# An encoder block on one core: merged moving operands in the block products, a last stage by token tile, and another order of the first loads

## The chip, the core and the metric

The kernel runs on one core of one Trainium2 chip. The metric is the device time of one execution in microseconds (us); the time given is the median of several runs. A profile is one execution, recorded instruction by instruction. Engines: PE is TensorE (matmuls) and PEld its weight loads, DVE is VectorE, ACT is ScalarE, POOL is GpSimd, SP is SyncE, which issues most DMAs.

## The reference, cut to what matters

```python
def reference(x, norm_mix, w_in, ..., norm_ffn, w_gate, w_up, w_down, norm_final):
    h = rmsnorm(x, norm_mix)                 # x: 512 tokens x 2048
    z = h @ w_in                             # Fourier part a, gMLP parts u and v
    ...
    x = x + concatenate([y_f, y_g]) @ w_out
    h2 = rmsnorm(x, norm_ffn)
    x = x + (silu(h2 @ w_gate) * (h2 @ w_up)) @ w_down    # d_ff = 5632
    return rmsnorm(x, norm_final)
```

Everything is float32. The weights `w_gate`, `w_up` (2048 x 5632) and `w_down` (5632 x 2048) carry most of the work.

## The kernel before

**Precision.** A float32 product is made of three matmuls in a reduced type (fp32r). Each operand is split into `hi` (a cast by ACT, L173) and `lo` (the rest, a subtraction by DVE, L174); then hi times hi, lo times hi and hi times lo are added up in one PSUM bank. So every weight tile of 128 x 1024 costs ACT one cast and DVE one subtraction, whatever is done with it.

**Stages, in order of time.** The input projections, the two mixers and the output projection (to about 560 us). Then the feed-forward part, an item list that `drive` (L925) walks: 16 plain gate and up units (`GateUp`); 16 pairs of **block products** (`Matrix`, `Block`: one gate matrix, one up matrix a pair, 32 of the 44 feature tiles); the rest of the gate and up units mixed with 140 `Product` items, the block products of the down projection, whose results POOL's DMA adds into DRAM (L818, `accum_op=ALU.add`); and at the end the down projection's last four feature tiles, done plainly (`Last` and the loop behind `drive`), with the final norm.

**A block product** works on a 2 x 2 cut of one matrix with seven products in place of eight (Strassen's scheme in Winograd's form). Sums of weight blocks are made by DVE in place (`sums`, L629), four a matrix, from four loaded blocks (L626). A product has 8 contraction tiles, and in each the three matmuls of `mm3b` (L700 to L702) with 256 moving columns, a token half: 24 matmuls. `out` (L661) takes the 256 columns of PSUM and combines them in the tiles `u`, `w` and `o`; at a pair's end `o` is scaled by the norm (L683, L685), passed through a silu and multiplied (L686), and stored by POOL's DMA (`keep`, L527).

**Order.** SP's, PE's, DVE's, ACT's and POOL's queues are written by hand in the feed-forward part: they hold the instructions in the order in which `drive` calls the items. At an item x, `drive` first makes the weight sums of the item three ahead (`sums`), then casts and splits the weights of the item two ahead (`prep`), issues loads further ahead (`load_ahead`), then calls `later` and `late` of the items before, then x's matmuls (`run`) and x's PSUM work (`out`). The `hi` and `lo` tiles have three buffers each, so a cast waits for PE to finish the item three earlier.

**The opening.** SP's queue holds the first half of the first activation tile, `g_mix`, then the first half of the first weights, and so on. ACT squares and casts in the order that a scheduler found.

**The end.** `Last(n)` multiplies one of the last two down units with all four token tiles and DVE adds the four results to x (L844). Then, token tile by token tile, the last unit is added (L970), squared with a row sum (L459), multiplied by the final gain (POOL, L973; the very last on DVE) and, when the row sums are there, by the inverse root (L112 to L118, L981, L983).

## Time and profile before

| | |
|---|---|
| median of 3 runs | 1850.15 us (1849.55 to 1850.80) |
| the profiled execution's own time | 1850.23 us |
| its span, first to last instruction | 1848.5 us |
| PE busy | 1820.0 us (98%), 10674 matmuls |
| DVE busy | 1407.4 us (76%) |
| ACT busy | 785.0 us (42%) |
| DMA, hardware queue | 209.83 MB, 33.7% of 16 engines |
| DMA, software (POOL) queue | 57.68 MB, 15.2% of 16 engines |

A matmul's duration in the trace is its way through the array; matmuls overlap, so what one costs is read from the distance of two starts. PEclk is the granted TensorE clock; 1.00 is the 2.4 GHz level. A row of a timeline gives start, duration, engine, line, operation and tiles, and in brackets the idle time of the engine before it with what ended it.

### The profile page before, as it was taken

The page shows a single profiled execution, that of the slowest core. Times are in us where ns is not written, and L with a number is a line of the kernel's source. Part 1 is how long each engine was busy: PE and PEld are TensorE (multiplying, and loading weights), DVE is VectorE, ACT ScalarE, POOL GpSimd, SP SyncE. Part 2 cuts the span into 40 slices and gives each one's busy share as a digit, 9 for nine tenths or more (in the row PEclk, how much of TensorE's full clock was granted, in tenths as well). Part 3 has the DMA queues.
Part 4 walks back from the last instruction along what each step waited for, and adds up shares of the span by engine and source line. Part 5 has one row for each costly group of instructions (what it writes and reads, how often), then busy time and mean ns, then how long its engine had stood idle before and what let it go on. Part 6 is the DMA issues. An engine that isn't in the chain of part 4 may idle for free.

```text
span 1848.5 us, 26416 instructions
## 1 busy us (share of the span) xinstructions
PE 1820.0 (98%) x10674; PEld 1614.0 (87%) x10674; DVE 1407.4 (76%) x1683; ACT 785.0 (42%) x1014; POOL 152.5 (8%) x160
## 2 busy tenths in 40 slices
PE   9999999999999999999999999999999999999996
PEld 7888888888888999999999999988888788788785
DVE  7554664333578888888888888889899898899957
ACT  6345533222333444443444444444445455444534
POOL 5001110000000000000000000001111111111104
PEclk9999999999999999999999999999999999999998
DMA  6322224442342343333334333338888878788672
GB/s 244 99 70 95 98 80 137 137 144 95 116 175 86 111 140 115 116 133 107 104 117 137 113 124 128 138 126 205 205 220 206 211 197 208 177 224 210 119 248 111
DMA packets 75577, 269.18 MB, mean 146 GB/s; under 512 B 8768, under 2 KB 8896, under 8 KB 75456
## 3 DMA queue, kind: packets, MB, share of 16 engines
q1 hardware_dynamic: 59616, 209.83, 33.7%
q0 software_dynamic: 15840, 57.68, 15.2%
q8 instruction: 83, 1.36, 0.3%
q14 instruction: 38, 0.31, 0.0%
HBM read 206.66 MB, written 60.82 MB: 145 GB/s over the span
## 4 chain that ended last, share of the span: by engine, by line
PE 89%; DVE 7%; issue 2%; ACT 1%; DMA 0%; POOL 0%; SPq 0%; ACTq 0%; DVEq 0%
PE upb L702 6%; PE upb L700 6%; PE upb L701 6%; PE gb L702 6%; PE gb L701 6%; PE gb L700 6%; PE d L790 5%; PE d L791 5%; PE d L789 5%; PE o L87 3%; PE o L85 3%; PE o L86 3%; PE g L87 2%; PE g L86 2%; PE g L85 2%; PE up L87 2%
## 5 line engine op out<-in xcount | busy, mean ns | idle before, releaser
L790 PE MATMUL d<-lo_d,X 128*128 128x512 f32 x560 | 219.4, 392 | 4.0 <-DVE lo_d L174 4.0
L789 PE MATMUL d<-hi_d,X 128*128 128x512 f32 x560 | 218.1, 389 | 2.4 <-DVE c L812 2.4
L791 PE MATMUL d<-hi_d,X 128*128 128x512 f32 x560 | 218.1, 389 | 0.0
L173 ACT CAST hi_d<-w 128x1024 fp32r<-128x1024 f32 x140 | 147.4, 1053 | 152.2 <-PE d L791 45.7
L174 DVE TENSOR_TENSOR lo_d<-w,hi_d 128x1024 fp32r<-128x1024 f32 x140 | 170.8, 1221 | 28.2 <-ACT hi_d L173 28.1
L173 ACT CAST hi_gb<-w_gb 128x1024 fp32r<-128x1024 f32 x112 | 117.5, 1049 | 150.0 <-PE upb L701 43.7
L173 ACT CAST hi_upb<-w_upb 128x1024 fp32r<-128x1024 f32 x112 | 117.5, 1050 | 135.4 <-PE gb L701 46.6
L174 DVE TENSOR_TENSOR lo_upb<-w_upb,hi_upb 128x1024 fp32r<-128x1024 f32 x112 | 136.8, 1221 | 37.3 <-ACT hi_upb L173 37.3
L174 DVE TENSOR_TENSOR lo_gb<-w_gb,hi_gb 128x1024 fp32r<-128x1024 f32 x112 | 136.7, 1221 | 34.4 <-ACT hi_gb L173 34.4
L702 PE MATMUL gb<-hf,lo_gb 128*128 128x256 f32 x512 | 145.0, 283 | 0.5 <-DVE lo_gb L174 0.5
L701 PE MATMUL gb<-hf,hi_gb 128*128 128x256 f32 x512 | 145.0, 283 | 0.4 <-DVE hf L174 0.4
L700 PE MATMUL gb<-hf,hi_gb 128*128 128x256 f32 x512 | 144.9, 283 | 0.0
L700 PE MATMUL upb<-hf,hi_upb 128*128 128x256 f32 x512 | 144.9, 283 | 0.0
L701 PE MATMUL upb<-hf,hi_upb 128*128 128x256 f32 x512 | 144.9, 283 | 0.0
L702 PE MATMUL upb<-hf,lo_upb 128*128 128x256 f32 x512 | 144.9, 283 | 0.0
L790 PEld LDWEIGHTS d<-lo_d,X 128*128 128x128 f32 x560 | 105.1, 188 | 30.8 <-DVE lo_d L174 9.3
L789 PEld LDWEIGHTS d<-hi_d,X 128*128 128x128 f32 x560 | 105.1, 188 | 25.1 <-ACT hi_up L173 2.0
L791 PEld LDWEIGHTS d<-hi_d,X 128*128 128x128 f32 x560 | 105.1, 188 | 21.3
L80 DVE TENSOR_TENSOR lo_o<-raw_o,hi_o 128x1024 fp32r<-128x1024 f32 x32 | 39.2, 1226 | 102.4 <-ACT hi_o L79 102.4
L700 PE MATMUL gb<-h2hi,hi_gb 128*128 128x256 f32 x384 | 108.8, 283 | 0.8 <-ACT t_gb L666 0.8
L702 PE MATMUL gb<-h2hi,lo_gb 128*128 128x256 f32 x384 | 108.8, 283 | 0.5 <-DVE lo_gb L174 0.5
L700 PE MATMUL upb<-h2hi,hi_upb 128*128 128x256 f32 x384 | 108.7, 283 | 0.0
(322 smaller groups left out, 4981.3 us busy)
## 6 DMA issues: line engine op xcount, KB each, us to landing
w<-in_w_down SPq DMA_DIRECT2D x80, 512.0 KB, 5.7
cd<-c POOLq DMA_DIRECT2D x80, 512.0 KB, 7.2
w_gb<-in_w_gate SPq DMA_DIRECT2D x64, 512.0 KB, 4.1
w_upb<-in_w_up SPq DMA_DIRECT2D x64, 512.0 KB, 4.4
raw_o<-in_w_out SPq DMA_DIRECT2D x32, 512.0 KB, 3.5
raw_g<-in_w_gate SPq DMA_DIRECT2D x24, 512.0 KB, 6.6
raw_up<-in_w_up SPq DMA_DIRECT2D x24, 512.0 KB, 6.8
ac<-ad SPq DMA_DIRECT2D x20, 512.0 KB, 3.6
```

The source lines that it names most:

```text
L80: nc.vector.tensor_sub(lo[:, c], raw[:, c], hi[:, c])
L85: mm(ps, lhs[0], rhs[0], start=first, stop=False)
L86: mm(ps, lhs[0], rhs[1], start=False, stop=False)
L87: mm(ps, lhs[1], rhs[0], start=False, stop=last)
L173: nc.scalar.copy(dst[0], src)
L174: nc.vector.tensor_sub(dst[1], src, dst[0])
L700: mm(ps, lhs[0], rhs[0], start=first, stop=False, skip_group_check=True)
L701: mm(ps, lhs[0], rhs[1], start=False, stop=False, skip_group_check=True)
L702: mm(ps, lhs[1], rhs[0], start=False, stop=last, skip_group_check=True)
L789: mm(p, X[:, 0, j, l], hi, start=j == 0 and not more, stop=False, skip_group_check=True)
L790: mm(p, X[:, 0, j, l], lo, start=False, stop=False, skip_group_check=True)
L791: mm(p, X[:, 1, j, l], hi, start=False, stop=j == 1, skip_group_check=True)
```

## The change

It does three things.

1. **Block products.** The hi and lo halves of an activation block now lie side by side in one tile, and one matmul streams both past the weights' hi part: 512 columns, hi times hi in the first 256, hi times lo of the activation in the second. The weights' lo part still takes 256. So 16 matmuls a product, and PSUM results of 512 columns, whose two halves are added only when all seven products are combined (in `out` of product 4 and in `fold`). The products run in another order (`BORDER`), and two of the four weight sums a matrix are made by DMA: a block is loaded a second time and POOL's DMA adds another block to it.
2. **The end.** The eight last down units (`Kept`) are all loaded and split ahead, beside the last gate and up units; both units of a token tile and column block are added up in one PSUM bank, the norm of a token tile runs beside the matmuls of the next, and for the last tile the multiplication by the gain goes ahead of the norm.
3. **The opening.** The first activation half and `g_mix` are issued from ACT's queue, ACT's first operations stand in a written order, and the first 12 matmuls go by operand half instead of by token tile.

The activation pool is laid out as KT tiles of twice the size, and the reserve for POOL's DMA descriptors is 4096 instead of 8192.

```diff
-    hpool = ctx.enter_context(tc.tile_pool(name="h", bufs=2 * KT))
+    hpool = ctx.enter_context(tc.tile_pool(name="h", bufs=KT))
...
-    nc.sync.dma_start(xrs[0][:, 0, :], a["xT"][0][:, 0, :])
-    nc.sync.dma_start(g_mix, a["norm_mix"])
+    nc.scalar.dma_start(xrs[0][:, 0, :], a["xT"][0][:, 0, :])
+    nc.scalar.dma_start(g_mix, a["norm_mix"])
...
+            if begin:
+                with tc.manual_schedule(engines={mybir.EngineType.SP, mybir.EngineType.Activation}):
+                    per_k(0)
+                    hi, lo = weights(units[kk], f"{name}_{kk}", 2)
...
+                    for x, y in ((0, 0), (0, 1), (1, 0)):
+                        for m in range(NT):
+                            mm(pss[m], h[x][:, m * P : (m + 1) * P], rhs[y], start=x + y == 0, stop=False)
...
     ORDER = (1, 6, 2, 7, 5, 4, 3)
+    BORDER = (1, 5, 2, 6, 7, 3, 4)
...
-            for k in {1: (11, 12, 22), 6: (21,)}.get(self.i, ()):
+            for k in {1: (11, 15), 5: (22,), 2: (21, 37)}.get(self.i, ()):
                 m.r[k] = slot(f"w{k}_{m.name}")
-                nc.sync.dma_start(m.r[k], m.src[k])
+                nc.sync.dma_start(m.r[k], m.src[{15: 11, 37: 12}.get(k, k)])
+                if k in (15, 37):
+                    nc.gpsimd.dma_start(m.r[k], m.src[12 if k == 15 else 22], accum_op=ALU.add)
...
-            if i == 1:
-                add(r[12], r[12], r[22])
-            elif i == 6:
-                add(r[11], r[11], r[12])
-            elif i == 7:
-                add(r[21], r[21], r[11])
-            elif i == 5:
-                sub(r[11], r[11], r[22])
...
+            if i == 6:
+                nc.vector.tensor_add(r[15], r[15], r[22])
+            elif i == 4:
+                nc.vector.tensor_add(r[21], r[21], r[15])
...
-                mm3b(ps, (self.hi[:, c], self.lo[:, c]), forms[i, j], j == 0 and not more, j == KT // 2 - 1)
+                x = forms[i, j]
+                mm(ps, self.hi[:, c], x, start=j == 0 and not more, stop=False, skip_group_check=True)
+                mm(ps[:, :H], self.lo[:, c], x[:, 0, :], start=False, stop=j == KT // 2 - 1, skip_group_check=True)
...
+            elif i == 5:
+                nc.scalar.copy(o(1, 1), ps)
...
             elif i == 7:
                 nc.vector.tensor_add(w, ps, u)
-            elif i == 5:
-                nc.vector.tensor_sub(o[:, 1, H:], ps, w)
...
+                nc.vector.tensor_sub(o(1, 1), o(1, 1), w)
+            elif i == 3:
+                nc.vector.tensor_sub(o(1, 0), ps, u)
...
+                nc.vector.tensor_add(o(0, 1), ps, w)
                 if not m.up:
...
+                    for f in range(2):
+                        to = g[:, f, :].rearrange("p (a b) -> p a b", b=H)
+                        nc.vector.tensor_add(to, m.o[f][:, :, 0, :], m.o[f][:, :, 1, :])
+                    nc.vector.tensor_mul(g, g, rg.unsqueeze(1).to_broadcast([P, 2, S]))
                 else:
...
+                    self.fold(0)
+
+        def fold(self, f):
+
+            halves = rg.rearrange("p (a b) -> p a b", b=H)
+            x = self.m.o[f][:, :, 0, :]
+            nc.vector.tensor_add(x, x, self.m.o[f][:, :, 1, :])
+            nc.vector.scalar_tensor_tensor(x, x, 0.5, halves, op0=ALU.mult, op1=ALU.mult)
+            to = pgu["o"][:, f, :].rearrange("p (a b) -> p a b", b=H)
+            nc.vector.tensor_mul(to, to, x)
 
         def late(self):
...
+            elif self.i == 4:
+                self.fold(1)
+                acts[self.m.p] = pgu["o"]
+                keep(self.m.p)
...
-        if n == len(units) - END + 1:
+        if n == len(units) - 2:
             items.append(Outputs())
...
+    beside = {-5: kept[:1], -4: kept[1:3], -3: kept[3:6], -2: kept[6:7], -1: kept[7:]}
...
+        for m in range(NT):
+            if m == 0:
+                for n in range(4):
+                    down(0, m, n)
+            for n in range(4):
+                if m:
+                    down(0, m, n)
+                down(1, m, n)
+                add(m, n)
+                if m and n == 0:
+                    root(m - 1)
+                elif m and n < 3:
+                    scale(m - 1, 2 * n - 2)
+                    scale(m - 1, 2 * n - 1)
...
-    nc = bacc.Bacc("TRN2", target_bir_lowering=False, num_devices=1, dynamic_dma_scratch_size=8192)
+    nc = bacc.Bacc("TRN2", target_bir_lowering=False, num_devices=1, dynamic_dma_scratch_size=4096)
```

In the new last stage `down` multiplies one unit with one token tile into the bank of (m, n), `add` adds the bank to x on DVE and squares on ACT, `root` makes the inverse root of one token tile, and `scale` multiplies by it and by the gain in one DVE instruction and stores.

PE's queue, in a gate block product before: two contraction tiles of product 1. `h2hi`, `h2lo` are the halves of the activation, `hi_gb`, `lo_gb` those of the weights, the last number is the moving columns.

```order
L700 MATMUL gb_1_7455<-h2hi_3001,hi_gb_1_7377 128x256
L701 MATMUL gb_1_7455<-h2lo_3002,hi_gb_1_7377 128x256
L702 MATMUL gb_1_7455<-h2hi_3001,lo_gb_1_7378 128x256
L700 MATMUL gb_1_7455<-h2hi_3010,hi_gb_1_7377 128x256
L701 MATMUL gb_1_7455<-h2lo_3011,hi_gb_1_7377 128x256
L702 MATMUL gb_1_7455<-h2hi_3010,lo_gb_1_7378 128x256
```

The same product now, three contraction tiles; `h` holds both halves.

```order
L676 MATMUL gb_1_7101<-h_0_2674,hi_gb_1_7036 128x512
L677 MATMUL gb_1_7101<-h_0_2674,lo_gb_1_7037 128x256
L676 MATMUL gb_1_7101<-h_1_2682,hi_gb_1_7036 128x512
L677 MATMUL gb_1_7101<-h_1_2682,lo_gb_1_7037 128x256
L676 MATMUL gb_1_7101<-h_2_2690,hi_gb_1_7036 128x512
L677 MATMUL gb_1_7101<-h_2_2690,lo_gb_1_7037 128x256
```

Two matmuls of 256 columns became one of 512; where there were three matmuls a contraction tile there are two.

DVE's queue where a pair ends and the next begins, before. `upb_4` and `upb_5` are PSUM results of the up matrix, `lo_gb_6` the weights' lo part for product 6 of the next gate matrix, `w_gb` weight blocks.

```order
L676 TENSOR_TENSOR o_upb_5423<-upb_4_5578,t_upb_5424 128x256
L174 TENSOR_TENSOR lo_gb_6_5605<-w_gb_5382,hi_gb_6_5604 128x1024
L678 TENSOR_TENSOR o_upb_5423<-upb_5_5547,t_upb_5424 128x256
L685 SCALAR_TENSOR_TENSOR o_upb_5423<-o_upb_5423,rstdB 128x1024
L686 TENSOR_TENSOR o_gb_5198<-o_gb_5198,o_upb_5423 128x1024
L174 TENSOR_TENSOR lo_gb_2_5643<-w_gb_5420,hi_gb_2_5642 128x1024
L637 TENSOR_TENSOR w_gb_5420<-w_gb_5420,w_gb_5382 128x1024
L639 TENSOR_TENSOR w_gb_5382<-w_gb_5382,w_gb_5386 128x1024
L174 TENSOR_TENSOR lo_gb_7_5679<-w_gb_5384,hi_gb_7_5678 128x1024
```

The same place now (line numbers of the changed kernel).

```order
L189 TENSOR_TENSOR lo_gb_5_5996<-w_gb_5824,hi_gb_5_5995 128x1024
L701 TENSOR_TENSOR o_upb_5858<-upb_4_6004,t_upb_5860 128x512
L716 TENSOR_TENSOR o_upb_5858<-o_upb_5858 128x2x256
L717 SCALAR_TENSOR_TENSOR o_upb_5858<-o_upb_5858,rstdB 128x2x256
L719 TENSOR_TENSOR g_gb_5845<-g_gb_5845,o_upb_5858 128x512
L656 TENSOR_TENSOR w_gb_5824<-w_gb_5824,w_gb_5855 128x1024
L189 TENSOR_TENSOR lo_gb_2_6027<-w_gb_5883,hi_gb_2_6026 128x1024
L716 TENSOR_TENSOR o_upb_5859<-o_upb_5859 128x2x256
L717 SCALAR_TENSOR_TENSOR o_upb_5859<-o_upb_5859,rstdB 128x2x256
L719 TENSOR_TENSOR g_gb_5845<-g_gb_5845,o_upb_5859 128x512
L189 TENSOR_TENSOR lo_gb_6_6058<-w_gb_5824,hi_gb_6_6057 128x1024
L189 TENSOR_TENSOR lo_gb_7_6085<-w_gb_5885,hi_gb_7_6084 128x1024
```

Between two `lo` parts there stand one weight sum instead of two, and two folds of three instructions in place of the scaling and the product.

DVE's queue at the program's end, before: from the last addition to x.

```order
L970 TENSOR_TENSOR x_1_15922<-l_3_3_16414,x_1_15922 128x512
L973 TENSOR_TENSOR o_1_16380<-x_1_15922,gB_16187 128x512
L977 TENSOR_REDUCE fs<-fss 128x1
L113 TENSOR_SCALAR rsq_fin_16426<-fs 128x1
L114 RECIPROCAL rsq_fin_16426<-rsq_fin_16426 128x1
L115 TENSOR_TENSOR rsq_fin_16426<-rsq_fin_16426 128x1
L116 TENSOR_TENSOR rsq_fin_16426<-rsq_fin_16426 128x1
L117 RECIPROCAL rsq_fin_16426<-rsq_fin_16426 128x1
L118 TENSOR_SCALAR fr<-rsq_fin_16426 128x1
L983 TENSOR_SCALAR o_0_16379<-o_0_16379,fr 128x512
L983 TENSOR_SCALAR o_1_16380<-o_1_16380,fr 128x512
```

And now.

```order
L1008 TENSOR_REDUCE fin_14796<-fss 128x1
L1009 TENSOR_SCALAR fin_14796<-fin_14796 128x1
L1010 TENSOR_TENSOR x_1_14436<-l_3_14783,x_1_14436 128x512
L1049 TENSOR_TENSOR o3b<-x_1_14436,gB_14477 128x512
L1019 SCALAR_TENSOR_TENSOR fin_14796<-fss,fin_14796 128x1
L1020 RECIPROCAL fin_14796<-fin_14796 128x1
L1021 SCALAR_TENSOR_TENSOR fin_14796<-fin_14796 128x1
L1022 RECIPROCAL fin_14796<-fin_14796 128x1
L1057 TENSOR_SCALAR o3a<-o3a,fin_14796 128x512
L1057 TENSOR_SCALAR o3b<-o3b,fin_14796 128x512
```

The row sum of the first three column blocks moved ahead of the last addition, and behind it four small instructions are left instead of seven.

## Rows read from the trace of the kernel before

**Rows 1.** Stretches: busy us (instructions) by engine, granted clock, DMA share, GB/s.

```profile
core 0: us, PE busy (x) PEld busy (x) DVE busy (x) ACT busy (x) POOL busy (x), PEclk, DMA share, GB/s
...
600.00:1200.00 600.00, 600.00 (x5002) 600.00 (x5002) 514.75 (x536) 249.96 (x283) 8.01 (x15) 1.00 0.37 122
...
1300.00:1780.00 480.00, 474.70 (x2075) 387.90 (x2074) 429.86 (x511) 224.12 (x281) 62.60 (x74) 1.00 0.80 201
```

**Rows 2.** Timeline of PE, matmuls of 512 columns; 20 rows between are left out.

```profile
300.06 0.39 PE L85 MATMUL u<-hhi,hi_u 128*128 128x512 f32 x1
...
304.82 0.39 PE L85 MATMUL o<-hi_o,yf 128*128 128x512 f32 x1
```

**Rows 3.** Timeline of PE, matmuls of 128 columns; seven rows between are left out.

```profile
242.82 0.28 PE L87 MATMUL sv<-wsps_hi,vn_lo 128*128 128x128 f32 x1
...
243.71 0.28 PE L86 MATMUL sv<-wsps_lo,vn_hi 128*128 128x128 f32 x1
```

**Rows 4.** Timeline of DVE where a pair ends (the place of the order above).

```profile
739.00 0.42 DVE L678 TENSOR_TENSOR o_upb<-upb,t_upb 128x256 f32<-128x256 f32 x1
739.45 1.23 DVE L685 SCALAR_TENSOR_TENSOR o_upb<-o_upb,rstdB 128x1024 f32<-128x1024 f32 x1
740.71 1.23 DVE L686 TENSOR_TENSOR o_gb<-o_gb,o_upb 128x1024 f32<-128x1024 f32 x1
741.85 1.22 DVE L174 TENSOR_TENSOR lo_gb<-w_gb,hi_gb 128x1024 fp32r<-128x1024 f32 x1
```

**Rows 5.** Timeline of DVE, operations of 512 columns.

```profile
1790.19 0.69 DVE L559 SCALAR_TENSOR_TENSOR s<-up,rstdB 128x512 f32<-128x512 f32 x1 [3.31 <-PE up L87]
1790.91 0.69 DVE L560 TENSOR_TENSOR act<-act,s 128x512 f32<-128x512 f32 x1
...
1795.53 2.48 DVE L844 TENSOR_TENSOR x<-l,x 128x512 f32<-128x512 f32 x4
```

**Rows 6.** Groups, 1300 to 1700 us: 512 columns read as two strided halves of 256.

```profile
L744 DVE TENSOR_TENSOR x<-ac,ac 128x512 f32<-128x512 f32 x7 | 4.8, 684 | 0.0
```

**Rows 7.** Timeline of PE and ACT around the same pair's end.

```profile
738.78 0.28 PE L700 MATMUL gb<-h2hi,hi_gb 128*128 128x256 f32 x1
...
738.90 1.05 ACT L173 CAST hi_gb<-w_gb 128x1024 fp32r<-128x1024 f32 x1 [1.08 <-PE upb L701]
```

**Rows 8.** DMA queues, 600 to 1200 us: packets, MB, share of 16 engines.

```profile
q1 hardware_dynamic: 17705, 64.48, 33.3%
```

**Rows 9.** DMA, 1300 to 1700 us: the software queue, and KB and landing of its additions.

```profile
q0 software_dynamic: 8966, 32.67, 45.6%
...
cd<-c POOLq DMA_DIRECT2D x61, 512.0 KB, 7.2
```

**Rows 10.** Timeline of the end: last matmul, last addition, and what follows.

```profile
1833.28 0.39 PE L87 MATMUL l<-dl_hi,al 128*128 128x512 f32 x1
...
1839.61 0.68 DVE L970 TENSOR_TENSOR x<-l,x 128x512 f32<-128x512 f32 x1
...
1842.44 0.15 DVE L118 TENSOR_SCALAR fr<-rsq_fin 128x1 f32<-128x1 f32 x1
1842.69 1.33 ACT L981 ACTIVATE o<-o,fr 128x512 f32<-128x512 f32 x2 [1.06 <-DVE fr L118]
```

**Rows 11.** Timeline of the opening, to the first real matmul.

```profile
0.74 0.38 SPq L124 DMA_DIRECT2D xr<-in_xT  x1
...
1.65 0.42 SPq L76 DMA_DIRECT2D raw_a<-in_w_a  x1
...
3.46 0.63 ACT L138 ACTIVATE acc<-xr 128x512 f32<-128x512 f32 x1 [1.44 <-DMA xr<-in_xT]
...
4.96 0.62 ACT L79 CAST hi_a<-raw_a 128x512 fp32r<-128x512 f32 x1 [0.88 <-DMA raw_a<-in_w_a]
5.49 0.72 ACT L134 ACTIVATE hhi<-xr,g_mix 128x512 fp32r<-128x512 f32 x1
...
6.26 0.50 PE L85 MATMUL a<-hi_a,hhi 128*128 128x512 f32 x1 [1.01 <-ACT hhi L134]
```

More of the change, by code (lines that the diff above doesn't have):

```diff
@@ L508, in encoder_block @@
     class RawUnit(Item):
+        early = False
         def __init__(self, src, name):
@@ L650, in run @@
             if i == 1:
-                m.o = slot(f"o_{m.name}", F32, (P, 2, S)) if m.up else wpool.tile([P, 2, S], F32, tag="raw", name=f"o_{m.name}")
-                m.t = small.tile([P, 3, H], F32, tag="t", bufs=1, name=f"t_{m.name}")
+                m.o = [wpool.tile([P, 2, 2, H], F32, tag="raw", name=f"o{f}_{m.name}") for f in range(2)]
+                m.t = small.tile([P, 2, S], F32, tag="t", bufs=1, name=f"t_{m.name}")
             more = i in (2, 3)
-            m.r["ps", i] = m.r["ps", {2: 1, 3: 5}[i]] if more else bank(f"{m.name}_{i}")
@@ L879, in encoder_block @@
             m = Matrix(p, up)
-            items += [Block(m, i) for i in ORDER]
+            items += [Block(m, i) for i in BORDER]
     units = units[4 * (FIRST + BLOCKS) :]
@@ L887, in encoder_block @@
         items.append(GateUp(*x))
+        items[-1].early = n < 3
         if n == len(units) - 8:
@@ L949, in drive @@
                     z.sums()
+                if k - len(works) == -6:
+                    for w in kept:
+                        w.load()
+                for w in beside.get(k - len(works), ()):
+                    w.prep()
                 load_ahead(k + 4)
@@ L956, in drive, with last_tile, last_stage, down @@
             before, last = last, x
+    def last_tile(name):
+        t = hpool.tile([P, 2, S], F32, tag="h", name=name)
+        return [t[:, 0, :], t[:, 1, :]]
+    def last_stage():
+        gB = []
+        for i in range(2):
+            for t in last_tile(f"gB{i}"):
+                c = slice(len(gB) * S, (len(gB) + 1) * S)
+                nc.sync.dma_start(t, a["norm_final"][:, c].partition_broadcast(P))
+                gB.append(t)
+        for t in gB:
+            nc.scalar.mul(t, t, 2.0)
+        ps, o, sums = {}, {}, {}
+        def down(i, m, n):
+            if i == 0:
+                ps[m, n] = bank(f"l{m}_{n}")
+            w = kept[4 * i + n]
+            for j in range(2):
+                c = slice(j * S, (j + 1) * S)
+                lhs = both(rest[2 * i + j], slice(m * P, (m + 1) * P))
+                mm3(ps[m, n], lhs, (w.hi[:, c], w.lo[:, c]), i + j == 0, i + j == 2)
+        def add(m, n):
+            if n == 3:
+                b = sums[m] = small.tile([P, 5], F32, tag="fin", name=f"fin{m}")
+                nc.vector.tensor_reduce(b[:, 0:1], fss[:, m, 0:3], axis=mybir.AxisListType.X, op=ALU.add)
+                nc.vector.tensor_scalar(b[:, 0:1], b[:, 0:1], 1.0 / D, EPS, op0=ALU.mult, op1=ALU.add)
+            nc.vector.tensor_add(xc(m, n), ps[m, n], xc(m, n))
+            squares(m, n, fss[:, m, n : n + 1], xc)
+        def root(m):
+            b = sums[m]
+            t, var, r = b[:, 1:2], b[:, 2:3], b[:, 3:4]
+            q = fss[:, m, 3:4]
+            nc.scalar.activation(t, q, AF.Sqrt, bias=b[:, 0:1], scale=1.0 / D)
+            nc.vector.scalar_tensor_tensor(var, q, 1.0 / D, b[:, 0:1], op0=ALU.mult, op1=ALU.add)
+            nc.vector.reciprocal(r, t)
+            nc.vector.scalar_tensor_tensor(var, var, r, t, op0=ALU.mult, op1=ALU.add)
+            nc.vector.reciprocal(b[:, 4:5], var)
+            o[m] = last_tile(f"o{m}a") + last_tile(f"o{m}b") if m < NT - 1 else o[m]
+        def store(m, n, queue=None):
+            (queue or nc.sync).dma_start(out[m * P : (m + 1) * P, n * S : (n + 1) * S], o[m][n])
+        def scale(m, n):
+            nc.vector.scalar_tensor_tensor(o[m][n], xc(m, n), sums[m][:, 4:5], gB[n], op0=ALU.mult, op1=ALU.mult)
+            store(m, n)
+        for m in range(NT):
[12 more added lines that the diff above has]
+                    scale(m - 1, 2 * n - 1)
+                if m == NT - 1:
+                    if n == 0:
+                        o[m] = last_tile(f"o{m}a") + last_tile(f"o{m}b")
+                    nc.vector.tensor_mul(o[m][n], xc(m, n), gB[n])
+        m = NT - 1
+        root(m)
+        r = sums[m][:, 4:5]
+        for n in range(4):
+            if n % 2:
+                nc.scalar.mul(o[m][n], o[m][n], r)
+            else:
+                nc.vector.tensor_scalar_mul(o[m][n], o[m][n], r)
+            store(m, n, nc.scalar if n == 3 else None)
```

140 lines of the change are left out of this document (50 added, 90 removed).

## The prediction, made before the changed kernel ran

> **What bounds the kernel now.** I read the stretches first, since the shares on the page mix stages. In the block products PE has no idle time at all (600.00 of 600.00 us) at a granted clock of 1.00, while DVE is busy 514.75 and the DMA engines 37% [rows 1]. So there the time is the number of matmuls by what one costs. In the later stage of down products PE still has 474.70 of 480 us with DVE at 429.86, 90%, and the DMA engines at 80% [rows 1]: that shows how near DVE and DMA may come to full before PE loses much, and the change pushes the block stage towards it.
>
> A matmul's duration overlaps the next one's, so I take starts. With 256 moving columns: 5002 matmuls in 600.00 us [rows 1], 0.120 us each. With 512: 21 steps from 300.06 to 304.82 [rows 2], 0.2267 us each. At the 2.4 GHz level 256 columns stream in 0.1067 and 512 in 0.2133 us; both costs lie 13.3 ns above that. So a matmul pays its columns and a fixed 13.3 ns. With 128 columns the step is 0.111 us (8 from 242.82 to 243.71) [rows 3], more than their 0.0533 + 0.0133: there the weight load sets the pace, and it is still under 0.120. Loads do not bind at 256 columns.
>
> **Part 1, the matmuls.** A contraction tile had three matmuls of 256 columns, 3 x 0.120 = 0.360 us. It now has one of 512 and one of 256: 0.2267 + 0.120 = 0.3467. The columns are the same; one fixed cost of 13.3 ns is gone. There are 32 matrices x 7 products x 8 tiles = 1792 of them, all on the path: 1792 x 13.3 ns = **-23.9 us**. The trace has no 512 followed by 256, so this is a bound from rows on either side: the load for the long matmul must fit beside the short one, and 0.111 under 0.120 says it does.
>
> The Trainium skill, "TensorE: Matmul & The Clock Gate", section "Back-to-back issue gap", gives N/2.4 + 2.5 ns for a warm matmul. By it a tile would go from 3 x 109.2 to 215.8 + 109.2 ns, and the change would save 2.5 ns a tile, 4.5 us in all. The trace does not agree: its fixed part is 13.3 ns at both widths.
>
> **Part 1, DVE.** A product shrinks to 8 x 0.3467 = 2.77 us, and DVE must keep up. Before, a pair had 26 operations of 1024 columns (14 lo parts, 8 sums, 4 of the gate) at 1.22 and 10 of 256 at 0.42 [rows 4]: 35.9 us. Now 20 of 1024 (14, 4, 2) and 18 of 512 at 0.69 [rows 5] (10 of PSUM results, 8 that add halves and gate): 36.8, over a pair of 38.8 instead of 40.3 us. Since neighbours overlap a little, that is near the 90% of the down products. What counts is the burst where matrices meet. Steps between DVE starts: 1024 columns 1.14 us, or 1.26 if the next reads the result [rows 4]; 512 columns 0.60 (four in 2.48, the last 0.69 long), or 0.72 if it reads the result [rows 5]; strided halves cost the same 684 ns [rows 6]. DVE begins 0.22 us after the next item's first matmul [rows 4, 7]. ACT's cast begins 0.12 after it and takes 1.05 [rows 7], early enough everywhere below.
>
> With T the start of a new pair, DVE's row in the order runs: addition T+0.22, the fold's three at 0.94, 1.67 and 2.39, weight sum 2.99, lo for product 2 at 4.13, done 5.35. PE wants it in the third item (two items on, 2 x 2.77) about 0.1 after its start, since the hi matmul comes first: 5.65. In time. Then the second fold at 5.27, 5.99, 6.71, and lo for product 6 at 7.31, done 8.53; wanted at 3 x 2.77 + 0.1 = 8.42. Late by 0.11, and with a hand-over of 0.06 (an item's last matmul starts 0.12 before T and takes 0.28, so it ends at T+0.16, and DVE starts at T+0.22) PE waits **0.17 us**. At a gate matrix's end: addition 0.22, halves 0.94 and 1.54, scaling 2.26, sum 3.40, lo for product 2 at 4.54, done 5.76 against 5.65: again 0.17. So 2 x 16 x 0.17 = **+5.4 us**. Bounds: nothing, if PE wants lo 0.2 later; or, if each independent step costs as a dependent one, 0.36 more at each place, +17. I take the middle value since its steps are measured ones.
>
> **Part 1, DMA.** Two of four sums move to DMA: a pair now loads ten blocks instead of eight and has four additions by POOL's queue. A load costs 33.3% of 600 us over 64.48 MB, 123 transfers of 0.524 MB, so 1.62 us of all engines [rows 8]. An addition into DRAM costs 45.6% of 400 us over 62 transfers, 2.93 us [rows 9]; into SBUF the trace has none, and I take this row, the only addition there is. A pair needs 10 x 1.62 + 4 x 2.93 + a store of some 1.3 = 29.2 us of 39.2, 75%, below the 80% that the down products bear. Latency: a doubled block goes load, wait, addition. The tightest tile (11 plus 12 of the next gate matrix) gets its buffer about 9.7 us into a pair, when a lo part has been made; with a landing of 5 us and 0.9 + 7.2 for the addition [rows 9] it is ready near 23, and its cast comes 13 items in, at 36. That slack of 13 us is the cover; on POOL's queue only the store of the finished pair stands behind such a wait, and nobody reads it soon. Cost: **0**, and beyond 13 us each late microsecond would stop ACT's casts and then PE.
>
> **Part 2, the end.** The last matmul ends at 1833.28 + 0.39 = 1833.67, but DVE's last addition starts only at 1839.61: six microseconds of backlog behind the first three token tiles' norms. The last ACT scaling ends at 1842.69 + 1.33 = 1844.02, the span at 1848.5 [rows 10]. From PE's end to the span's end: 14.8 us. Now: no POOL multiplications beside DVE, half the additions, and each tile's norm beside the next tile's 10.9 us of matmuls, so the backlog is gone. Behind the last matmul: addition 0.73, square and row sum 0.85, root 0.35, four small operations 0.65, scaling 1.4: 4.0, then the stores as before, 4.5 less 0.1, since one of four is issued from ACT. 8.4 instead of 14.8: **-6.4 us**. Bounds -4.5 (two microseconds of backlog stay) and -7.5. The matmuls before it are as many as before; eight splits beside the last five items (27 us of PE) and loads of x issued later have several items of cover. If that were gone, PE has eight banks and could run four results ahead.
>
> **Part 3, the opening.** The first weights stand third on SP's queue, at 1.65 us behind 0.74; now they are first: 0.91 earlier. They gate the cast at 4.96, hhi at 5.49 and the first matmul at 6.26 [rows 11]. The activation's cast now goes ahead (xr is there at 3.46), so after the weights' cast PE starts near 5.35: **-0.9 us**, between 0 (the loads share the same engines) and -1.3.
>
> **The sum**, against the profiled execution's 1850.2 (span 1848.5 and 1.7 around it; the median is 1850.15): 1850.2 - 23.9 + 5.4 - 6.4 - 0.9 = 1824.4.
>
> **Rivals.**
> - *DVE takes most of it.* Dependent steps everywhere, +17 instead of 5.4: 1836; a little more at other meeting points, up to 1846. For it: DVE's 90%, and the late points are hundredths from fitting. Against: measured steps, and idle time between bursts. 0.14.
> - *The fixed cost does not go.* If the two halves of the merged operand each paid it, a tile stayed at 0.360, the items were as long as before and DVE in time: 1850.2 - 6.4 - 0.9 = 1842.9. Against: both widths show the same 13.3 ns. 0.05. By the page named above the saving is 4.5 us, 1838.4.
> - *Slower: additions by DMA become the bound.* If an addition into SBUF costs twice the DRAM row, 5.9 us, a pair needs 16.2 + 23.5 + 1.3 = 41.0 us of DMA, 2.2 over PE's 38.8; 16 x 2.2 = 35: 1850.2 - 23.9 + 35 - 7.3 = 1854. It decides from about 5.6 us an addition. For it: no such row; the landing is already 7.2 us. Against: 2.93 with DRAM on both ends of the write. 0.07.
> - *The end keeps its length* (another engine's backlog in place of DVE's): 1831, inside the range.
>
> **How the numbers follow.** Forecast, 1816 to 1833: 0.74. Its low end is no stall, -7.5 and -1.3 and a microsecond where the block stage begins. The range goes on to 1838 to take in half of the first rival: 1816 to 1838, with some 0.82. Faster by more than 0.2% (about what a measurement of this kernel can tell) means below 1846.5: 0.74 + 0.13 + 0.04 = 0.91; within: 0.02, the far ends of the first two rivals; slower: 0.07.
>
> **What would show it.** Starts of a 512 and a 256 matmul 0.227 and 0.120 apart; PE idle some 0.2 us twice a pair, ended by a lo part of product 6 or 2; DVE near 90% and DMA near 75% from 600 to 1180 us, and no wait of ACT for a POOL addition; the last addition within 0.1 us of the last matmul, 8 to 9 us before the span's end; the first matmul near 5.4. Wrong would make it: PE waits of a microsecond at each matrix, or casts that wait for DMA.

## The result, and the profile after

The changed kernel takes 1831.51 us (median; 1831.32 to 1831.79) beside 1850.09 of the kernel before: a ratio of 0.990, 95% interval 0.9886 to 0.9914. The profiled execution took 1831.4 us. That is 18.6 us faster; the forecast was 25.8 faster (1850.2 to 1824.4), and its range, 1816 to 1838, holds the time. The direction is right, and one large term has the wrong size. The stretches, as in [rows 1]:

```profile
core 0: us, PE busy (x) PEld busy (x) DVE busy (x) ACT busy (x) POOL busy (x), PEclk, DMA share, GB/s
600.00:1200.00 600.00, 600.00 (x3407) 521.33 (x3406) 537.19 (x578) 284.49 (x322) 59.36 (x74) 1.00 0.71 197
1300.00:1780.00 480.00, 474.14 (x2072) 387.01 (x2071) 425.75 (x504) 227.69 (x285) 59.99 (x71) 1.00 0.81 206
```

PE is busy for all of the first stretch at the full granted clock, exactly as before, and this row alone would say that nothing is left to look for. The count says more: 3407 matmuls, two to a tile, are 1703.5 tiles in 600 us, 352.2 ns each. Forecast were 346.7. A matmul's row is longer (0.39 and 0.28 us) than the step to the next, so the rows overlap, and neither a slower step nor a wait of 0.15 us shows as idle time of PE. Starts show both. From the timeline of PE, two places of the same kernel:

```profile
667.54 0.39 PE L676 MATMUL gb<-hf,hi_gb 128*128 128x512 f32 x1
667.77 0.28 PE L677 MATMUL gb<-hf,lo_gb 128*128 128x256 f32 x1
667.88 0.39 PE L676 MATMUL gb<-hf,hi_gb 128*128 128x512 f32 x1
668.11 0.28 PE L677 MATMUL gb<-hf,lo_gb 128*128 128x256 f32 x1
668.23 0.39 PE L676 MATMUL gb<-hf,hi_gb 128*128 128x512 f32 x1
...
622.33 0.40 PE L676 MATMUL gb<-h,hi_gb 128*128 128x512 f32 x1
622.57 0.28 PE L677 MATMUL gb<-h,lo_gb 128*128 128x256 f32 x1
622.68 0.40 PE L676 MATMUL gb<-h,hi_gb 128*128 128x512 f32 x1
622.92 0.28 PE L677 MATMUL gb<-h,lo_gb 128*128 128x256 f32 x1
623.04 0.40 PE L676 MATMUL gb<-h,hi_gb 128*128 128x512 f32 x1
623.28 0.28 PE L677 MATMUL gb<-h,lo_gb 128*128 128x256 f32 x1
623.39 0.40 PE L676 MATMUL gb<-h,hi_gb 128*128 128x512 f32 x1
```

At 667 us two tiles take 0.69 us, 346.7 ns each: the forecast. At 622 three tiles take 1.06, 353.3 each, with long steps that repeat every three tiles (232, 240, 236 ns). There are two paces. The time of a whole product (16 matmuls, start to start, in ns) tells them apart; here are three pairs of the changed kernel, gate matrix and up matrix, in the order 1, 5, 2, 6, 7, 3, 4:

```
pair 7   2819 2830 2831 2819 2830 2831 2819 | 2830 2831 2836 2831 2819 2830 2831
pair 10  2773 2773 2774 2961 2831 2819 2830 | 2831 2819 2815 2774 2773 2773 2774
pair 11  2773 2773 2774 2958 2830 2831 2819 | 2830 2831 2842 2831 2819 2830 2831
```

2773 is 8 x 346.7. The 2961 and 2958 are product 6 of a gate matrix, one of the two places at which the forecast put a wait. This is how one looks (weight loads of PE, the same place in pair 4):

```profile
743.21 0.19 PEld L676 LDWEIGHTS gb<-hf,hi_gb 128*128 128x128 f32 x1
743.59 0.19 PEld L677 LDWEIGHTS gb<-hf,lo_gb 128*128 128x128 f32 x1 [0.20 <-DVE lo_gb L189]
743.70 0.19 PEld L676 LDWEIGHTS gb<-hf,hi_gb 128*128 128x128 f32 x1
```

A load that should start 0.11 after the one before starts 0.38 after it, released by the lo part. From 600 to 1180 us the waits of the weight loads, in us in total, times, and the longest:

```profile
PEld gb L677 <- DVE lo_gb L189: 0.8, 4, 0.2
PEld upb L677 <- DVE lo_upb L189: 0.6, 3, 0.2
```

Seven waits, of some thirty forecast. Of the 224 products 165 run at the longer pace, 50 at 2773 (three of these, in which the pace turns, take 2787), and 9 hold a wait (two of them at the entry of the stage). The whole stage, first matmul to the first behind it, takes 634.0 us: 224 x 2.7733 = 621.2, and 8.85 of longer pace, and 3.9 of waits (2.6 of it at the entry).

The rest of the forecast's signs. DVE is busy 537.19 of 600 us, 90%, as forecast. DMA has 71% (forecast 75%), in two queues:

```profile
q1 hardware_dynamic: 21033, 76.58, 36.9%
q0 software_dynamic: 10528, 38.34, 34.7%
```

(the two queues from 600 to 1180 us: packets, MB, share of the engines; [rows 8] had the first).

The end, answering to [rows 10]:

```profile
1820.09 0.39 PE L89 MATMUL l<-hi_dk,al 128*128 128x512 f32 x1
...
1820.59 0.68 DVE L1010 TENSOR_TENSOR x<-l,x 128x512 f32<-128x512 f32 x1
...
1823.72 0.71 ACT L1055 ACTIVATE o3b<-o3b,fin 128x512 f32<-128x512 f32 x1
1824.46 0.35 ACTq L1026 DMA_DIRECT2D out_dram<-o3b  x1
```

The last addition starts 0.11 us behind PE's end (1820.09 + 0.39), not six: the backlog is gone. From PE's end to the span's end (1829.4) it is 8.9 us. The opening, answering to [rows 11]:

```profile
0.74 0.41 ACTq L126 DMA_DIRECT2D xr<-in_xT  x1
...
5.44 0.63 ACT L140 ACTIVATE acc<-xr 128x512 f32<-128x512 f32 x1 [2.49 <-DMA xr<-in_xT]
6.23 0.72 ACT L136 ACTIVATE h<-xr,g_mix 128x512 fp32r<-128x512 f32 x1 [0.17 <-DMA g_mix<-in_norm_mix]
6.86 1.12 ACT L81 CAST hi_a<-raw_a 128x512 fp32r<-128x512 f32 x2
...
7.51 2.07 PE L169 MATMUL a<-hi_a,h 128*128 128x512 f32 x4 [2.50 <-ACT hi_a L81]
```

The first matmul starts at 7.51, not at 5.4: ACT waits for xr until 5.44, where it had it at 3.46 before.

### The profile page after: what moved, and what is told of

It is laid out like the page before. It is cut to its first block, busy times and chain, and to the rows that moved or that the text cites. A ratio compares the mean times of both kernels' runs of the same rounds, so it can differ in the third digit from the quotient of the medians.

```text
span 1829.4 us, 23171 instructions
## 1 busy us (share of the span) xinstructions
PE 1806.3 (99%) x8882; PEld 1518.4 (83%) x8882; DVE 1409.3 (77%) x1704; ACT 811.7 (44%) x1044; POOL 188.6 (10%) x209
## 4 chain that ended last, share of the span: by engine, by line
PE 88%; DVE 6%; DMA 2%; issue 2%; ACT 1%; POOL 0%; ACTq 0%; DVEq 0%; SPq 0%
PE gb L676 11%; PE upb L676 11%; PE gb L677 6%; PE upb L677 6%; PE d L820 5%; PE d L821 5%; PE d L819 5%; PE o L89 3%; PE o L87 3%; PE o L88 3%; PE up L89 2%; PE up L87 2%; PE up L88 2%; PE g L89 2%; PE g L87 2%; PE g L88 2%
## 5 line engine op out<-in xcount | busy, mean ns | idle before, releaser
L676 PE MATMUL gb<-hf,hi_gb 128*128 128x512 f32 x512 | 181.8, 397 | 0.0
L676 PE MATMUL upb<-hf,hi_upb 128*128 128x512 f32 x512 | 181.4, 396 | 0.0
L676 PE MATMUL gb<-h,hi_gb 128*128 128x512 f32 x384 | 137.3, 397 | 0.9 <-ACT t_gb L688 0.9
L676 PE MATMUL upb<-h,hi_upb 128*128 128x512 f32 x384 | 137.7, 397 | 0.0
L676 PEld LDWEIGHTS upb<-hf,hi_upb 128*128 128x128 f32 x512 | 96.1, 188 | 23.2
L848 POOL DMA_DIRECT2D cd<-c x80 | 68.8, 860 | 449.6 <-ACT c L838 163.4
L676 PEld LDWEIGHTS gb<-hf,hi_gb 128*128 128x128 f32 x512 | 96.1, 188 | 22.8
```

The lines of the kernel that those rows point to most:

```text
L676: mm(ps, self.hi[:, c], x, start=j == 0 and not more, stop=False, skip_group_check=True)
L848: nc.gpsimd.dma_start(cd[self.np_, to // 10 - 1, to % 10 - 1], c, accum_op=ALU.add)
```

## Experiments

**One order of the matmuls instead of another.** Is the change of width what costs, or the merged matmul itself, or the columns that are added to? Three kernels with the same matmuls.

```diff
-            for j in range(KT // 2):
-                mm(ps, hi_j, x_j); mm(ps[:, :H], lo_j, x_j[0])
+            for j in range(KT // 2): mm(ps, hi_j, x_j)               # hi_then_lo
+            for j in range(KT // 2): mm(ps[:, :H], lo_j, x_j[0])
...
+                mm(ps[:, H:], lo_j, x_j[0])                          # lo_second_half
...
+            hi_0 lo_0 lo_1 hi_1 hi_2 lo_2 lo_3 hi_3 ...              # pairs_swapped
```

> The changed kernel, but in each block product all eight 512-column matmuls come first and then all eight 256-column ones; the same matmuls, another order. In the changed kernel a tile's two matmuls take 352 ns from start to start, not the 346.7 forecast, in a regular pattern (350, 361, 349, 347, 346). Theory A, a change of width costs, about 5.2 ns for the two changes of a tile: in rows of one width the steps are 226.7 and 120.0 again, a tile takes 347.3 in the mean, and 1792 x 4.6 ns = 8.2 us go: 1823.3 us. Theory B, the merged matmul itself costs 232 because its operand comes in two parts: steps of 232 in a row of eight, 1831.5 us. Beside that, the lo part is wanted 1.8 us later in a product, so waits for it should be none under both.

> The changed kernel, but the 256-column matmul adds into the second half of the result's columns and not the first; the two halves are added later in any case. Widths still alternate. Theory A, the change of width costs: 352 ns a tile as before, 1831.5 us. Theory C, the cost is that a matmul adds to columns that were written just before: the distance between two writes of the same columns changes at both joints (512 to 256 nearer, 256 to 512 farther), so the steps of 233 and 117 move, and the tile with them, to 346.7 or to above 355: 1822 or above 1837 us.

> The changed kernel, but every second tile has its 256-column matmul first: 512, 256, 256, 512, 512, 256, 256, 512. Half as many changes of width. Theory A: the mean tile is halfway, 349.3 ns, and 1792 x 2.6 ns = 4.7 us go: 1826.8 us. Theory B, the merged matmul costs 232 wherever it stands: 352 ns and 1831.5 us. Theory C, adding to columns just written: the joints 256 to 256 and 512 to 512 write the same columns as near as any, so 352 or more.

hi_then_lo takes 1824.06 us (ratio to before 0.9863, interval 0.9846 to 0.9879), lo_second_half 1829.9 and pairs_swapped 1830.2 (one run each). Stretches from 600 to 1180 us, of the changed kernel and of these three in turn:

```profile
600.00:1180.00 580.00, 580.00 (x3293) 503.97 (x3292) 519.33 (x560) 274.82 (x311) 59.36 (x74) 1.00 0.72 199
```
```profile
600.00:1180.00 580.00, 580.00 (x3326) 510.45 (x3325) 518.94 (x565) 276.35 (x313) 59.31 (x74) 1.00 0.73 202
```
```profile
600.00:1180.00 580.00, 580.00 (x3304) 505.01 (x3303) 521.00 (x561) 275.18 (x312) 59.35 (x74) 1.00 0.72 199
```
```profile
600.00:1180.00 580.00, 580.00 (x3313) 501.16 (x3312) 523.28 (x564) 275.28 (x313) 59.35 (x74) 1.00 0.73 200
```

The more matmuls in the same 580 us, the better the pace; DVE and DMA are alike in all four. With hi first, every undisturbed product of the stage takes 2793 ns, and no wait for lo is left. So theory B falls: the last steps of a row of eight are 227, and the merged matmul does not cost 232 wherever it stands. Theory A, whose total came near, falls as a price by the change: it put a product at 2778, and two changes leave 20 ns over 2773, and the eight of pairs_swapped leave 14 (2787 in every undisturbed product). lo_second_half has the two paces of the changed kernel, 2773 and 2819 to 2831, just as often mixed (103 and 103 products): where the columns lie does not matter, and theory C falls. What stays is that an order of widths has a pace of its own, and the strict alternation has two. The total of pairs_swapped says little of its pace: it still has 31 products that wait for lo (3.4 us over), and at the stage's entry it loses 4.0 us, where its granted clock stood at 0.5 from 583.7 to 587.0 us.

**The opening undone.**

```diff
-    nc.scalar.dma_start(xrs[0][:, 0, :], ...); nc.scalar.dma_start(g_mix, ...)
+    nc.sync.dma_start(xrs[0][:, 0, :], ...); nc.sync.dma_start(g_mix, ...)
...
-                    per_k(0)                       # activation ahead of the weights
-                    for x, y in ((0, 0), (0, 1), (1, 0)):   # k == 0: by kind, then by m
```

> The changed kernel with the opening of before (order of the first loads, activation cast behind the weights, matmuls in the order of before). In the changed kernel the first matmul starts at 7.51 us, not 6.26, and the block products 0.31 later. Theory A, the new opening costs 0.3 us: first matmul at 6.3, block products begin 0.3 earlier, 1831.2 us. Theory B, the 0.31 comes from the new tile of h (both parts in one buffer) and not from the order: first matmul earlier but the block products still begin at 574.6, 1831.5 us. By the forecast, it would have cost 0.9: 1832.4 us.

1828.87 us (1827.87 to 1829.72). The first matmul starts at 6.04 and the block products at 574.25 instead of 574.57: 0.3, as theory A has it, but the scatter told of below is larger, so these two traces alone decide nothing. The total fell by 2.6; in the profiled run the block stage happens to have 120 products at 2773 and takes 631.2 us instead of 634.0, with not one instruction of it changed. Over the traces of this study the 201st matmul behind the warm-up, ahead of which only the opening differs, starts at 53.4 to 55.8 us with the new opening (seven kernels, mean 54.5) and at 53.8 to 54.4 with the old one (six, mean 54.1): the new one gains nothing in the mean and scatters more.

The steps of the first real matmuls, 512 columns each, show where the scatter comes from (in ns, start to start):

```
changed kernel          584 427 427 426 427 427 426 379 230
old_end (same opening)  335 235 234 235 231 231 236 228 233
```

512 columns in 427 ns is the 1.2 GHz level. The changed kernel's granted clock from 9 to 11 us is 0.51 (columns as in [rows 1]):

```profile
9.00:11.00 2.00, 2.00 (x6) 1.61 (x5) 1.51 (x2) 2.00 (x4) 1.53 (x1) 0.51 1.03 412
```

PE had stood idle there for 2.5 us, between the warm-up matmuls and the first real one. With the new opening five of seven traces begin at this level, for 6 to 14 matmuls, and reach the 201st at 54.2 to 55.8 us. The other two, old_end and sums_on_dve, have steps of some 230 from the second on, like the old opening (one of its six traces has two longer ones), and reach it at 53.4, 0.7 ahead of the old opening's mean, though their first matmul starts at 7.3 too:

```profile
7.33 1.20 PE L169 MATMUL a<-hi_a,h 128*128 128x512 f32 x4 [1.65 <-ACT hi_a L81]
```

So by these traces what the new opening loses is the clock, not the later start. No run holds the clock and changes the opening alone.

**Both waits for lo taken away.** Two of DVE's steps are put later: the second fold, and a weight sum.

```diff
-        def late(self):                # up matrix: fold(1), ahead of lo of product 6
+        def later(self):               # behind it
...
+        def behind(self, y):           # weight sum for product 6 behind lo of product 2
+            return isinstance(y, Block) and y.m is self.m and (y.i, self.i) == (2, 6)
```

> The changed kernel with two steps of VectorE moved, and nothing else: the second fold of an up matrix (three 512-column operations) goes behind the lo part for product 6 of the next matrix, and the weight sum for product 6 behind the lo part for product 2. What the runs so far show: an undisturbed product takes either 2773 ns (8 x 346.7, as forecast) or 2820 to 2831, and changes from one to the other only after a wait of PE for lo in product 6 of a gate matrix or product 2 of an up matrix (147 to 189 ns, where the pace is 2773); in the changed kernel 165 of 224 products have the slow pace (8.85 us in all). Theory D, the pace is set where PE resumes after a wait: both waits go here (lo is ready 1.1 and 2.2 us earlier), so the pace after the entry of the stage is one and the same for all pairs: all at 2773 (block products 624 us, 1821.7 us in all) or all at about 2827 (636 us, 1833.5). Theory E, the pace is disturbed by other engines' work (casts, additions, DMA): the mix stays, 634 us, 1831 us.

Four runs: 1821.22, 1821.34, 1832.03 and 1832.77 us, the two values of theory D and nothing between. The profiled one is one of the long ones (span 1830.9):

```profile
600.00:1180.00 580.00, 580.00 (x3285) 503.49 (x3284) 511.86 (x557) 272.67 (x309) 58.34 (x73) 1.00 0.73 199
```

Not one weight load waits for lo in this stretch, and all 220 products behind the entry take 2819 to 2831 ns (3285 matmuls are 353.1 ns a tile). The short runs have no trace; that their products all run at 2773 is read from the total, which theory D gave as 1821.7. One program gives both times, so its order of work on DVE, ACT and DMA does not set the pace, and the two paces don't mix within the run, as theory E would have them: it falls. The clock doesn't set it either: the mean granted clock is 0.999 in the long runs and 0.997 in the short ones. The pace is kept as long as nothing holds PE up. In the traces of the changed kernel, old_opening and lo_second_half it changes 52 times behind the entry, either way, and each time in product 6 of a gate matrix or product 2 of an up matrix, the two whose lo part comes last, 49 to 217 ns behind the product's first matmul. A wait of some 0.19 us isn't needed for it: the turns from the longer pace to 2773 come with hold-ups of under 0.1 us, which the list of waits doesn't show.

**The end undone.**

```diff
-        last_stage()
+    # of before: Last and Tail items, additions by (m, n), products with gB on POOL
+    (nc.vector if final else nc.gpsimd).tensor_tensor(out=oc[n], in0=xc(m, n), in1=gB..., op=ALU.mult)
```

> The changed kernel with the end of before (the last down products by output columns, multiplications on POOL). Forecast for this part was -6.4 us; in the changed kernel the end from the last matmul's start to the span's end is 9.28 us against 15.18, 5.9 less, but a wait of 0.92 us for lo of the last up matrix is new. Theory A, the end is worth 5.9 - 0.8 = 5.1: 1836.6 us, with the last matmul some 15 us before the end of the span and that wait gone. Theory B, the end's backlog came from the old block products' order and is gone with them: 1831.5 or less. The pace of the block products can move the total by up to 4 us either way, so the stretch from the first of the last four tiles' matmuls to the span's end decides: 52.6 us in the changed kernel, 58.5 before.

1831.58 us in all, but by the stretch that decides: from the first matmul of the last four tiles to the span's end it takes 59.1 us (1770.7 to 1829.8) against 52.6 in the changed kernel and 58.5 before. Its last matmul starts at 1814.02 and the last addition only at 1820.36:

```profile
1818.80 1.35 POOL L1004 TENSOR_TENSOR o<-x,gB 128x512 f32<-128x512 f32 x1 [1.17 <-DVE x L1001]
...
1820.36 0.68 DVE L1001 TENSOR_TENSOR x<-l,x 128x512 f32<-128x512 f32 x1
```

Theory A: the end is worth 6.5 us in that stretch, and takes 1.0 back ahead of it (the stretch from the first down product to it is 557.3 in the changed kernel and 556.3 here). That the total is nonetheless that of the changed kernel is luck: its block stage takes 630.2 us instead of 634.0, and it begins 1.2 earlier, the opening at the full clock. The run shows the paces best, with the same block products: behind the entry 189 products run at 2773 and none at the longer pace, and the waits are there in every matrix, 15 and 15 of them from 600 to 1180 us.

```profile
PEld gb L677 <- DVE lo_gb L189: 2.9, 15, 0.2
PEld upb L677 <- DVE lo_upb L189: 2.8, 15, 0.2
```

```
pair 5   2773 2774 2773 2933 2774 2773 2773 | 2774 2773 2920 2773 2774 2773 2773
```

2933 and 2920: product 6 of the gate matrix and product 2 of the up matrix, 160 and 147 ns over, where the forecast had 170 and 170. A pair takes 39.13 us; forecast were 38.83 + 0.34 = 39.17.

**The weight sums back on DVE.**

```diff
-            for k in {1: (11, 15), 5: (22,), 2: (21, 37)} ...  # 15, 37 doubled by nc.gpsimd.dma_start(accum_op=add)
+            for k in {1: (11, 12), 5: (22,), 2: (21,)} ...
+            if i == 5: nc.vector.tensor_add(r[11], r[11], r[12])
+            elif i == 7: nc.vector.tensor_add(r[12], r[12], r[22])
...
+        def behind(self, y):           # weight sum for product 5 behind lo of product 1
```

> The changed kernel with all four weight sums of a matrix on VectorE again and no additions by DMA: four loads a matrix, 22 + 2 operations of 1024 columns a pair on VectorE instead of 20 and as many of 512. Theory A, VectorE is at its limit: by durations 24 x 1.22 + 18 x 0.69 = 41.7 us a pair against PE's 38.8, by starts 24 x 1.14 + 18 x 0.60 = 38.2; PE waits for lo in most matrices, a pair takes 40 to 41.7 us, and the time is 1840 to 1868 us. Theory B, VectorE's operations overlap enough: pairs of 39.1 to 39.6 as in the changed kernel, 1829 to 1834 us. DMA's share of the block stage falls from 72% to some 37% under both; if PE's pace came from the DMA traffic, it would be 2773 ns a product throughout where PE doesn't wait.

1864.1 us (one run), 14 slower than before and 33 slower than the changed kernel. Here PE does lose time that the busy share shows (the stretch from 600 to 1180 us), and its waits there name DVE (us in total, times, longest):

```profile
600.00:1180.00 580.00, 559.14 (x3123) 478.06 (x3123) 550.17 (x586) 259.75 (x293) 7.46 (x14) 1.00 0.34 115
```
```profile
PE gb L682 <- DVE lo_gb L189: 17.6, 14, 1.3
PE upb L682 <- DVE lo_upb L189: 2.9, 14, 0.2
```

Theory A, inside its range. DVE is at 95%, and PE loses 1.3 us at each product 6 of a gate matrix. DMA has 34% instead of 72%, and both paces are there (56 products at 2773, 116 at the longer), so the longer pace does not need the DMA traffic either. Without the two doubled tiles by DMA, in this order of DVE's steps, the merged matmuls would have made the kernel slower.

**lo last everywhere, and other rows.** The down products and the units of gate and up wait for lo as well (4.0 us for lo_d in the changed kernel), so lo goes last there too; then the block products in rows of two, of four, and alternating with lo two tiles behind (these three with the two DVE steps of dve_order as well).

```diff
+            for j in range(2):                              # down product
+                for t in range(2):
+                    for k in range(2): mm(ps[t], X[:, k, j, l[t]], hi[c[j]])
+            for t in range(2):
+                for j in range(2): mm(ps[t], X[:, 0, j, l[t]], lo[c[j]])
...
+            hi_0 hi_1 lo_0 lo_1 hi_2 hi_3 lo_2 lo_3 ...      # rows_of_2
+            hi_0 .. hi_3 lo_0 .. lo_3 hi_4 .. hi_7 lo_4 .. lo_7   # rows_of_4
+            hi_0 hi_1 lo_0 hi_2 lo_1 hi_3 ... hi_7 lo_5 lo_6 lo_7  # lagged
```

> The changed kernel with three edits: the block products with all hi matmuls first (as in hi_then_lo), the same in the down products and in the gate and up products by units (matmuls with lo last), and the opening of before. Expected from hi_then_lo's 1824.1: the opening gives 0.3 back; PE's waits for lo of the down products (4.0 us in 8 waits, each of at most 1.4) and of the gate and up units (0.9) go, since lo is wanted 1.8 us later: 1818.9 us. Rival, VectorE is late throughout there and not only in bursts: the waits come back later in each product, 1823.8 us.

> The kernel lo_last_old_opening (1819.2 us) with VectorE's two steps moved as in dve_order, and the block products' matmuls in rows of two: 512, 512, 256, 256, four times. Theory D, each order has a pace of its own as long as PE isn't stopped: this is the sequence of pairs_swapped shifted by one, which ran at 2787 ns a product against 2793 for rows of eight; without waits all products take 2787 and the time is 1819.2 - 224 x 6 ns = 1817.9 us, alike in every run. Theory F, a change of width has a fixed price, some 10 ns (two changes cost rows of eight 20 ns a product): eight changes, 2853 ns a product and 1832.6 us.

> As rows_of_2, in rows of four: 512 four times, 256 four times, twice. Theory D: between the rows of two and of eight, 2787 to 2793 ns a product and 1818 to 1819.5 us, alike in every run. Theory F: four changes, 2813 ns and 1823.7 us.

> As rows_of_2, but the widths alternate with lo two tiles behind: 512, 512, then six times 256 and 512, then 256, 256. Theory D: within the row the two paces of the alternation (346.7 or 353 ns a tile) are possible, but the start of a product is the same every time and no wait disturbs it, so that all products take the same time, 2773 to 2787 (1815 to 1818 us) or 2810 to 2830 (1823 to 1827 us), in every run alike. If the pace differs from run to run as in dve_order (1821 and 1832), the start of a product doesn't set it, but the entry of the stage. Theory F: twelve to fourteen changes, 2890 ns or more, above 1840 us.

lo_last_old_opening takes 1819.18 us (ratio 0.9833, 0.9819 to 0.9846); PE has no wait for lo_d left, while its waits for DVE's work on `c` in the same stage grew from 2.5 to 4.3 us. rows_of_2 takes 1818.88 (0.9826, 0.9810 to 0.9842), the fastest of the study and 12.6 us under the changed kernel; the two can't be told apart. rows_of_4 takes 1822.26 (0.9849) and lagged 1825.01 (0.9864). Their undisturbed products take, all alike from pair 1 to 15:

```
rows of 2 (and pairs_swapped)   2786 to 2787 ns
rows of 8 (hi_then_lo)          2793 to 2794
rows of 4                       2799 to 2801
lagged                          2818 to 2822
strict alternation              2773, or 2819 to 2831
```

Theory D holds in so far as all products of a trace have one pace. The other runs are known by their totals alone, which spread over 1.5 to 3.6 us, so that every run is alike is not shown. Theory F, a price by the change, would have had rows of 2 and lagged above 1832. Where D put rows of four, between two and eight, it was wrong: I know no rule that orders these numbers.

## Why the prediction was right or wrong, point by point

- **The fixed cost of a matmul (-23.9): right as a price, not as what was got.** A tile of 346.7 ns is there, to the nanosecond, in 47 products of the changed kernel and in 189 of old_end. The step that failed is "the trace has no 512 followed by 256, so this is a bound from rows on either side": it was taken as the value. The alternation has a second pace, 353 ns, and three quarters of the products ran at it: +8.85 us. That term is the miss, and nothing in the sum bounded it on the slow side. By the Trainium skill, "TensorE: Matmul & The Clock Gate", section "Back-to-back issue gap", an estimate of a tile is 325 ns (215.8 + 109.2); no kernel here has a product under 8 x 345, so the trace keeps disagreeing.
- **Waits for lo (+5.4): right in place and size, and mostly replaced.** lo for product 6 was forecast to be done 8.53 us into a pair; in pair 4 it is done at 743.54, 8.54 in. Where products take 2773 the two waits are 0.15 to 0.16 us. In the longer pace a product gives DVE 0.05 us more, so lo lands about 0.05 us behind the start of product 6 instead of 0.22, and the waits all but go: the two costs exclude each other. Of 5.4 us, 1.3 came. Together with the pace that makes +4.2 us over the forecast of the block stage (634.0 us, with 0.6 less at its entry). dve_order and old_end show both halves alone. That the time still fell into the first range, 1816 to 1833, is in part luck: the miss of the pace was half paid by the waits that it took away.
- **DMA (0): right for the block stage.** 72% of the engines' time. An addition into SBUF costs 3.1 us (the software queue's 34.7% of 580 us less 15 stores of 1.3, over 59 additions), beside the 2.93 taken from [rows 9], and ACT waits nowhere for one. The rival of DMA as the bound falls with that, and sums_on_dve shows what leaving the sums on DVE would have cost. (By the rival's own sum an addition would make DMA outlast PE's 38.8 us from 5.3 us on, and turn the sign from 5.8; "about 5.6" follows from neither.)
- **The end (-6.4): right, -5.9.** One thing had no place in the sum: SP issues the eight kept loads in one burst (1746.25 to 1751.66 us), and the last up unit's weights stand behind them. Issued at 1753.94, these land 15.3 us later (before, 9.4). ACT is idle for 6.69 us until they come, and DVE for 6.51, so it is the load that makes lo late, not the splits. PE waits 0.52 us for it, and the stretch ahead of the end grows by 0.8. "Several items of cover" counted the splits and the loads of x, and not this load.

```profile
1769.32 1.05 ACT L188 CAST hi_up<-raw_up 128x1024 fp32r<-128x1024 f32 x1 [6.69 <-DMA raw_up<-in_w_up]
1770.40 1.23 DVE L189 TENSOR_TENSOR lo_up<-raw_up,hi_up 128x1024 fp32r<-128x1024 f32 x1 [6.51 <-ACT hi_up L188]
1771.68 0.50 PE L89 MATMUL up<-h,lo_up 128*128 128x512 f32 x1 [0.52 <-DVE lo_up L189]
```

- **The opening (-0.9): wrong, +0.3.** I took xr to be there at 3.46 as before. It landed 4.7 us after its issue; that two queues now ask for it and for the weights at once is the likely reason, and no run moves it alone. And ACT's square of xr stands first in the trace, ahead of the activation's cast: the source writes it later, outside the written order, which I had read past. So the first matmul came at 7.51 and not near 5.4. What that cost is mostly the clock, which stood at 0.5 for the first matmuls; the sum had no such term. Where it didn't (old_end, sums_on_dve), the opening is 0.7 ahead of the old ones' mean, near the forecast.
- **The rivals.** "DVE takes most" named 1836 for a cause that did not act; the time came nearer to it by the pace. "The fixed cost doesn't go" is half true at the longer pace: 353.3 of 360 keep 6.7 of the 13.3 ns.

Sum: -25.8 + 4.2 (block stage) + 0.5 (end) + 0.8 (ahead of it) + 1.2 (opening) = -19.1, the difference of the spans (1848.5 to 1829.4).

What stays open: why the alternation has two paces, and what at a stop selects one. After a wait of the same length the long steps that follow are 234 to 239 ns where the pace stays at 2773, and 230 to 231 where it turns to the longer one; that is a trace of the choice, not its cause. The two outcomes lie a few ns apart: from the 2773 pace, lo for product 2 of an up matrix ended 206 to 208 ns behind the product's first matmul in 24 products in which the pace stayed (old_opening, lo_second_half, old_end), and 208, once 206, in 7 in which it turned.

## What to carry to other kernels

Read the pace of matmuls from starts and counts, not from the busy share, and take a step that no row shows as a range. Put what is late last within an item: with all hi matmuls ahead of lo, no wait for lo was left in the block products, and PE kept one pace. Alone that was worth 7.5 us, though a product took 2793 ns and not 2773; with the same order in the down products and the other units, and the opening of before, it was 12.3. Before judging an edit by its total, compare stage by stage: here an edit in the first 10 us or in the last 50 moved the total by 2 to 4 us through a stage that it did not touch.

## What the runs showed of the hardware

- Matmuls of 512 and 256 columns in strict alternation run at 346.7 or 353.3 ns a pair of them, at a granted clock of 1.00 in both; the pace changes only where a late operand holds PE up, for less than 0.1 us in some cases, and holds for up to 220 products (dve_order: 1821.2 or 1832.8 us from one program).
- Behind a change of width the steps are not yet those of a long stretch: the first eight steps of a product in hi_then_lo are 234, 236, 228, 232, 231, 227, 227, 226 ns, where [rows 2] have 227. The disturbance of a change lasts some five matmuls.
- Behind 2.5 us in which PE stood idle, the first matmuls of 512 columns took 427 ns each at a granted clock of 0.5 (changed kernel, 7.5 to 11 us), against 227 at 1.00. Behind 1.6 to 1.7 us of idle time the same opening shows either level (lo_second_half 427, old_end 230).
- A load of 512 KB behind a burst of eight others on one queue landed 15.3 us after its issue (changed kernel, 1753.94); in the kernel before, issued ahead of the first of these, it took 9.4.
- An addition by DMA into SBUF takes 3.1 us of all DMA engines for 512 KB, a load 1.46 (36.9% of 580 us over 147 loads).
